# Memory attention of the first layer one step earlier, and two tiles handled by halves

## The chip, the cores and the metric

The kernel runs on one core of a Trainium2 chip. A core has five engines that run side by side and wait for each other by semaphores: TensorE (PE in the profile; its weight loads are listed apart as PEld), VectorE (DVE), ScalarE (ACT), GpSimd (POOL) and SyncE (SP), which here only issues DMAs. TensorE reads its operands from SBUF and writes to PSUM, which has 8 banks of 128 x 512 float32. The metric is the device time of one execution in microseconds, lower is better.

## The reference

Two layers run over a residual stream of 512 tokens with 1024 features. Each layer has a token mixer, a cross-attention of 4 heads into 256 memory tokens beside it, one output projection for both, and a gated MLP with a short causal convolution. Layer 0 mixes by differential attention with 6 heads, layer 1 by gated linear attention. Cut to what the change touches, layer 0:

```python
h = rms_norm(x, attn_norm[i])
proj = h @ w_in_diff[j]                      # q, k, v, mem_q
mix = diff_attention(q, k, v, ...)           # 6 heads, two softmaxes each, o = (p0 - lam * p1) @ v
# memory_cross_attention(mem_q, mem, ...):
kv = rms_norm(mem, mem_norm_g) @ w_kv        # 256 memory tokens -> k, v
q = rms_norm(q, g0) * (64 ** -0.5); k = rms_norm(k, g1)
p = softmax(q @ k.T); cross = p @ v          # 4 heads of 64
x = x + concat([mix, cross]) @ w_out[i]
x = x + conv_ffn(rms_norm(x, ffn_norm[i]), w_up[i], conv_w[i], conv_b[i], w_down[i])
```

All is float32. Large products are made of three passes: each operand is split into a rounded part (hi) and a remainder (lo), and hi·hi, hi·lo and lo·hi are summed in PSUM.

## The kernel before

**Order of the work.** TensorE's instructions run exactly in the order in which the program writes them. The opening (lines 361 to 430) is also in written order on ScalarE, VectorE, GpSimd and SyncE. Everywhere else a planner orders the instructions of the other engines and of the DMA queues by its own estimate of when each becomes ready; an engine then works through its list strictly in that order, so an instruction that waits holds up all behind it.

**The filler.** `Filler` (line 92) holds small units of large projections. `F.fill(us)` takes units off the list for about so many microseconds, so that TensorE has work while a chain of attention runs through the other engines. `F.need(name)` takes units until a mark is reached. A unit of a projection is 6 matmuls (lines 257 to 259) of 512 columns.

**Weights.** SyncE loads weight tiles (line 212), ScalarE casts them to the hi part (line 203), VectorE subtracts for the lo part (line 206). Five such pairs are held at a time, so the cast of a later tile waits for the matmuls that read an earlier one.

**The opening.** The first projection goes by k, an eighth of the 1024 features at a time. For k = 0 one DMA of 128 x 512 float32 on ScalarE's queue (line 374) brings the first weights, VectorE casts them in one instruction (line 401), and x comes and is split in two halves of 256 tokens (lines 376 and 403). For k = 0 the 12 matmuls, four token blocks by three passes, go by pass: hi·hi of all four blocks first (lines 427 to 430).

**Layer 0's attention.** `diff_layer` (line 547) runs 21 steps t (line 689). A step works on one third of a head: steps 0, 3, 6 and so on take query blocks 2 and 0, the next block 1, the next block 3. In a step TensorE does the logits of t (line 615, two banks of the pool "lg"), the products with v of t - 2 (line 653, pool "sm"), a fill, the norms of the next pair of heads when t is 4 or 10 (lines 717 to 719), the turn of t - 1 (transposes, line 172, pool "tp"), pieces of the memory attention, a second fill, and then what the next heads need: `prepare` (line 574) turns queries and keys of a head in steps 5, 6, 11 and 12, `finish` (line 666) turns the output of a head. Each of the pools "lg", "sm", "tp" and "mm" has two banks.

After the logits VectorE adds the bias and finds the maximum (line 620; the bias tile bt comes by DMA, line 606), ScalarE takes the exponential (line 623), VectorE combines the two softmaxes (lines 628 to 631), and after the turn ScalarE copies the transposes out of PSUM (line 641).

**Memory attention.** `MemAttn` (line 483) has four query blocks. `logits(b)` writes two lg banks (line 506); VectorE finds the maxima (line 509), ScalarE the exponentials (line 513), VectorE the quotient (lines 515 and 517). `turn(u)` transposes half a block into a tp bank, copied out by VectorE or ScalarE in turn (line 526). `values(pair)` multiplies with v (line 540, an sm bank) and splits the result (lines 240 and 241). The constant M0 = 7 (line 688) places them: with m = t - M0, logits at m = 0 to 3, turns at m = 1 to 4, two in each, and values at m = 3 and 5. The memory keys are turned once by `keys0` (line 469), at the end of step 6 (line 735), through an lg bank, and copied out by ScalarE (line 475). Step 10 also makes the operands of the second layer's memory projection (lines 700 to 702, splits by lines 240 and 241).

**The end.** The last product of layer 1's MLP is made in tiles of 128 features by 512 tokens. VectorE adds each to the residual (line 995) and SyncE issues the DMA to the output (line 1093).

Of the kernel before, what the change touches and what calls it, by code (L numbers as in the profile page):

```python
# [131 lines left out]
def trunk(ctx, tc, head_d, x_t, mem_t, wpack, cols_a_d, cols_d, conv_d, gate_d, rel_bias, diff_lambda, consts, onehot, out):  # L132
# [12 lines left out]
    def bank(tag):  # L145
        return ps.tile([128, 512], F32, name=f"ps_{tag}", tag=tag)
# [12 lines left out]
    def blk(b, w=128):  # L159
        return slice(w * b, w * b + w)  # L160
# [200 lines left out]
    with tc.tile_pool(name="ini", bufs=1) as ip, tc.manual_schedule(engines={E.Activation, E.DVE, E.Pool, E.SP}):  # L361
        idle = ip.tile([128, 512], F32, name="idle")
        rb = ip.tile([32, 6], F32, name="rb")
        oh = ip.tile([32, 640], F32, name="oh")
        bs = xtile()[:6], xtile()[:6, :128]
        lv = xtile()[:, :256]
        G.memset(idle, 0.0)
        p = bank("tp")
        for n in (512, 320):
            mm(p[:, :n], idle[:, 0:128], idle[:, :n], start=True, stop=True)  # L370


        raws = [ip.tile([128, WTILE], F32, name=f"raw{i}") for i in range(4)]
        A.dma_start(raws[0][:, blk(0, S)], wpack[0, :, blk(0, S)])
        head = ip.tile([128, 32 + S], F32, name="head")
        for c in (slice(0, 32 + S // 2), slice(32 + S // 2, 32 + S)):
            load(head[:, c], head_d[:, c])
        xT[0] = head[:, 32:]
        for k in range(1, KT):
            xT[k] = xtile()  # L380
            load(xT[k], x_t[k])
            load(raws[k // 2][:, blk(k % 2, S)], wpack[k // 2, :, blk(k % 2, S)])
        load(cols_a, cols_a_d)
        at[0] = 4
        load(C[:, 640:768], consts[:, 640:768])
        load(rb, rel_bias)
        load(oh, onehot)
        second = [load_raw(raw_tile(), WTILE) for _ in range(3)]
        load(cols, cols_d)
        load(lv, diff_lambda[0].rearrange("a b -> (a b)").partition_broadcast(128))  # L390
        parts, acc, split_w = [], [None], [None]
        made.append(parts)

        def operands(k):
            if k % 2 == 0:
                split_w[0] = [wp.tile([128, WTILE], F32R, name=n, tag=n, bufs=WB) for n in ("whi", "wlo")]
            c = blk(k % 2, S)
            hi, lo = split_w[0]
            xh[k], xl[k] = split_tiles()
            if k == 0:  # L400
                V.tensor_copy(hi[:, c], raws[0][:, c])
                V.tensor_sub(lo[:, c], raws[0][:, c], hi[:, c].bitcast(F32))
                for t in (blk(0, S // 2), blk(1, S // 2)):
                    split(xh[0][:, t], xl[0][:, t], xT[0][:, t], col(0, head))
            else:
                split(xh[k], xl[k], xT[k], col(k, head))
                split_weights(c, raws[k // 2], hi, lo)
            parts.append((hi[:, c], lo[:, c]))
            squares(xT[k], acc)

        operands(0)
        for k in range(KT):
            if k + 1 < KT:
                operands(k + 1)
            if k == 0:
                second.append(load_raw(raws[0], WTILE))
            if k == 4:
                bias_rows(rb, oh, bs)
            if k == KT - 2:
                make_piece(second, lambda: token_rsqrt("lg", acc[0], NB, r_x[:, 0]))  # L420
                weights(("qk", 0))
                small_vectors()
                for c in range(2):
                    load(bias_d[:, 512 * c:min(512 * c + 512, 640)], bs[c])
            hi, lo = parts[k]
            terms = (xh[k], hi), (xh[k], lo), (xl[k], hi)
            todo = [(b, i) for b in range(NB) for i in range(3)]
            for b, i in sorted(todo, key=lambda bi: bi[1]) if k == 0 else todo:
                xp, w = terms[i]
                mm(first[b], xp[:, blk(b)], w, start=k == 0 and i == 0, stop=k == KT - 1 and i == 2)  # L430

    load(C[:, 0:640], consts[:, 0:640])
    for i in range(4):
# [16 lines left out]
    def mem_kv(l):  # L450
        hs, ls = [None] * KT, [None] * KT
        km = [None]

        def operands():
            if l == 0:
                mem_squares()
            km[0] = xtile().rearrange("p (b n) -> p b n", b=2)
            for k in range(KT):
                if k % 2 == 0:
                    mh, ml = split_tiles()  # L460
                c = blk(k % 2, 256)
                hs[k], ls[k] = mh[:, c], ml[:, c]
                split(hs[k], ls[k], memT[k // 2][:, c], c_mem(l, k))

        def ev(b, p):
            A.activation(km[0][:, b], p[:, :256], AF.Copy, scale=r_mem[:, b:b + 1])
            A.activation(vm[l][:, b], p[:, 256:], AF.Copy, scale=r_mem[:, b:b + 1])

        def keys():
            F.need(f"kv{l}")  # L470
            p = bank("lg")
            for hp in range(2):
                for b in range(2):
                    transpose(p[:, 256 * hp + 128 * b:256 * hp + 128 * b + 128], km[0][:, b, blk(hp)])
            A.activation(kmT[l].rearrange("p a b -> p (a b)"), p, AF.Copy, scale=c_mk(l))
        gemm(hs, ls, 2, ("kv", l), 512, ev,
             (lambda: token_rsqrt("lg", mem_acc[0], 2, r_mem)) if l == 0 else None)
        F.add(0.0, lambda: group_norm(None, km[0], 2, 4, 64))
        F.mark(f"kv{l}")
        return operands, keys  # L480


# [64 lines left out]
    def diff_layer(pool, mix, acc):  # L547
# [137 lines left out]
        F.fill(1.2)  # L685
        prepare(1)
        ma = MemAttn(pool, 0, qm, mix, False)
        M0 = 7
        for t in range(21):
            if t == 0:  # L690
                project_qk(1)
                ops0, keys0 = mem_kv(0)
                gemm(xh, xl, NB, ("v", 1), 512, lambda b, p: A.activation(
                    v12[:, b], p, AF.Copy, scale=r[:, b:b + 1]))
                F.mark("v1")
                project_qk(2)
            if t == 2:
                ops0()
                ma.norm()
            if t == 10:  # L700
                ops1, keys1 = mem_kv(1)
                ops1()
            if t == 16:
                keys1()
            if t == 12:
                load_x(x_t)
                out_proj(0, mix, 0, None)
            if t == 18:
                rest = out_proj(0, mix, 1, acc, 5)
            f = FILL[bisect(STEPS, t)]  # L710
            m = t - M0
            if t < 18:
                logits(t)
            if 0 <= t - 2 < 18:
                values(t - 2)
            F.fill(f)
            if t in (4, 10):
                norms((t + 2) // 6, 0)
                norms((t + 2) // 6, 1)
            if 0 <= t - 1 < 18:  # L720
                turn(t - 1)
            if 1 <= m < 5:
                ma.turn(2 * m - 2)
            if m in (3, 5):
                ma.values(m // 2 - 1)
            if 0 <= m < 4:
                ma.logits(m)
            if t == 20:
                F.flush()
            F.fill(f)  # L730
            if 1 <= m < 5:
                ma.turn(2 * m - 1)
            if t == 3:
                ma.queries()
            if t == 6:
                keys0()
            if t in (5, 6, 11, 12):
                prepare(2 * ((t + 1) // 6) + (t + 1) % 6)
            if t % 3 == 2 and t >= 5:
                finish(t // 3 - 1)  # L740
# [253 lines left out]
    def update(n, p, gain, acc):  # L994
        V.tensor_add(xT[n], xT[n], p)
        if gain is None:
            return
        xh[n], xl[n] = split_tiles()
        split(xh[n], xl[n], xT[n], gain(n))
        squares(xT[n], acc)  # L1000
# [27 lines left out]
    def ffn(pool, l, acc):  # L1028
# [31 lines left out]
        for half, nq in enumerate(HALVES):  # L1060
# [22 lines left out]
            for c in range(4):  # L1083
                pn = bank("lg"), bank("tp")
                parts = weights(("dn", l, base, c))
                for n in range(2):
                    product(pn[n], parts, n, mids)
                for n in range(2):
                    update(2 * c + n, pn[n], (lambda k: c_attn(1, k)) if last and l == 0 else None, acc2)
                    if last and l == 0:  # L1090
                        nc.sync.dma_start(xres[2 * c + n], xT[2 * c + n])
                    if last and l == 1:
                        nc.sync.dma_start(out[2 * c + n], xT[2 * c + n])
# [91 lines left out]
```

## Time and profile before

| | |
|---|---|
| median of 3 runs | 1187.88 us (1187.5 to 1188.62) |
| profiled execution | 1186.74 us |
| its span, first to last instruction | 1185.0 us |
| TensorE busy | 1171.4 us (99%), 5656 matmuls |
| VectorE busy | 756.9 us (64%) |
| ScalarE busy | 546.2 us (46%) |
| DMA | 117.81 MB, mean 99 GB/s |
| mean granted TensorE clock | 0.998 |

How to read the rows: L615 is line 615 of the kernel. A row of the order of time gives start, duration, engine, line, operation, output<-inputs, shapes and the number of instructions merged; in brackets, for how long the engine stood idle before and who ended that. A row of the waits reads "engine, its line <- engine and line waited for: us in total, times, longest". A row of the stretches gives the stretch, its length, then busy time (and instructions) of PE, PEld, DVE, ACT and POOL, the granted clock as a share of full speed, the DMA share and GB/s. A row of DMA issues ends with the size and the median us from issue to landing. Durations of neighbouring matmuls overlap, since they are pipelined.

### The profile page before, as it was taken

How to read it: one execution, taken by the hardware profiler on the slowest of the kernel's cores; microseconds unless marked ns; L12 is line 12 of the kernel's file. 1: busy time of each engine (PE TensorE's matmuls, PEld its weight loads, DVE VectorE, ACT ScalarE, POOL GpSimd, SP SyncE). 2: the span in 40 equal slices, each digit the busy share in tenths (PEclk: the TensorE clock that was granted, in tenths of full speed). 3: DMA queues.
4: the chain of work that ended last, by engine and by line, in shares of the span. 5: the costliest groups of instructions: out<-in, count | busy, mean ns of one | idle time of the engine just before them, and what ended most of it. 6: DMA issues, size and time to landing. Idle time of an engine off the chain costs nothing.

```text
span 1185.0 us, 14743 instructions
## 1 busy us (share of the span) xinstructions
PE 1171.4 (99%) x5656; PEld 966.8 (82%) x5656; DVE 756.9 (64%) x1250; ACT 546.2 (46%) x952; POOL 4.5 (0%) x25
## 2 busy tenths in 40 slices
PE   9999989999999999999999999999999999999998
PEld 7888867888888888888888788988888888888887
DVE  7566686687767435767557746768777643476741
ACT  6676676564434223444437535436443422343420
POOL 0000000000000000000000000000000000000000
PEclk9999999999999999999999999999999999999999
DMA  8432214142322332322341221333233233242231
GB/s 294 126 93 89 80 41 138 49 139 72 124 89 89 107 107 80 116 71 90 119 152 68 72 71 59 110 99 125 72 111 102 76 120 107 71 125 72 89 116 44
DMA packets 39268, 117.81 MB, mean 99 GB/s; under 512 B 4671, under 2 KB 6520, under 8 KB 39198
## 3 DMA queue, kind: packets, MB, share of 16 engines
q1 hardware_dynamic: 39054, 116.62, 30.9%
q8 instruction: 44, 0.72, 0.3%
q10 hardware_dynamic: 144, 0.26, 0.1%
q14 instruction: 26, 0.21, 0.1%
HBM read 112.65 MB, written 4.21 MB: 99 GB/s over the span
## 4 chain that ended last, share of the span: by engine, by line
PE 93%; DVE 3%; ACT 2%; issue 1%; DMA 0%; ACTq 0%; DVEq 0%
PE ps_mm L275 9%; PE ps_mm L276 9%; PE ps_mm L274 9%; PE ps_sm L275 7%; PE ps_sm L274 7%; PE ps_sm L276 7%; PE ps_mm L257 5%; PE ps_mm L259 5%; PE ps_mm L258 5%; PE ps_tp L275 3%; PE ps_tp L274 3%; PE ps_tp L276 3%; PE ps_lg L275 3%; PE ps_lg L276 3%; PE ps_lg L274 3%; PE ps_tp L172 2%
## 5 line engine op out<-in xcount | busy, mean ns | idle before, releaser
L203 ACT CAST whi<-raw 128x1024 fp32r<-128x1024 f32 (+4 forms) x212 | 208.4, 985 | 261.1 <-PE ps_tp L275 131.2
L206 DVE TENSOR_TENSOR wlo<-raw,whi 128x1024 fp32r<-128x1024 f32 (+4 forms) x212 | 241.1, 1140 | 107.5 <-ACT whi L203 106.4
L274 PE MATMUL ps_mm<-xsh,whi 128*128 128x512 f32 x438 | 173.0, 395 | 0.0
L275 PE MATMUL ps_mm<-xsl,whi 128*128 128x512 f32 x438 | 170.6, 390 | 0.2 <-DVE xsl L241 0.2
L276 PE MATMUL ps_mm<-xsh,wlo 128*128 128x512 f32 x438 | 170.7, 390 | 0.0
L274 PE MATMUL ps_sm<-xsh,whi 128*128 128x512 f32 x378 | 147.1, 389 | 0.0
L276 PE MATMUL ps_sm<-xsh,wlo 128*128 128x512 f32 x378 | 147.1, 389 | 0.0
L275 PE MATMUL ps_sm<-xsl,whi 128*128 128x512 f32 x378 | 147.1, 389 | 0.0
L257 PE MATMUL ps_mm<-whi,xsh 128*128 128x512 f32 (+2 forms) x352 | 136.2, 387 | 0.1
L259 PE MATMUL ps_mm<-whi,xsl 128*128 128x512 f32 (+2 forms) x352 | 131.0, 372 | 0.4 <-DVE xsl L241 0.4
L258 PE MATMUL ps_mm<-wlo,xsh 128*128 128x512 f32 (+2 forms) x352 | 130.6, 371 | 0.0
L1045 ACT ACTIVATE cvo<-u,cv 128x512 f32<-128x512 f32 x88 | 71.4, 813 | 121.4 <-DVE u L1043 121.4
L275 PEld LDWEIGHTS ps_mm<-xsl,whi 128*128 128x128 f32 x438 | 82.3, 188 | 17.6 <-DVE xsl L241 0.6
L274 PEld LDWEIGHTS ps_mm<-xsh,whi 128*128 128x128 f32 x438 | 82.3, 188 | 17.4 <-issue 0.5
L276 PEld LDWEIGHTS ps_mm<-xsh,wlo 128*128 128x128 f32 x438 | 82.2, 188 | 17.1
L1046 DVE SCALAR_TENSOR_TENSOR cvo<-u,cv,cvo 128x512 f32<-128x512 f32 x88 | 65.8, 749 | 38.7 <-ACT cvo L1045 38.7
L274 PEld LDWEIGHTS ps_sm<-xsh,whi 128*128 128x128 f32 x378 | 71.0, 188 | 14.8
L275 PEld LDWEIGHTS ps_sm<-xsl,whi 128*128 128x128 f32 x378 | 71.0, 188 | 14.7
L276 PEld LDWEIGHTS ps_sm<-xsh,wlo 128*128 128x128 f32 x378 | 70.9, 188 | 14.7
L257 PEld LDWEIGHTS ps_mm<-whi,xsh 128*128 128x128 f32 x352 | 66.4, 189 | 13.6 <-issue 3.0
L259 PEld LDWEIGHTS ps_mm<-whi,xsl 128*128 128x128 f32 x352 | 66.1, 188 | 12.5 <-DVE xsl L241 0.6
L258 PEld LDWEIGHTS ps_mm<-wlo,xsh 128*128 128x128 f32 x352 | 66.4, 189 | 10.0
(271 smaller groups left out, 1746.4 us busy)
## 6 DMA issues: line engine op xcount, KB each, us to landing
raw<-in_wpack_dram SPq DMA_DIRECT2D x178, 512.0 KB, 3.5
xt<-in_x_t_dram SPq DMA_DIRECT2D x15, 256.0 KB, 6.0
raw<-in_wpack_dram SPq DMA_DIRECT2D x15, 256.0 KB, 3.9
raw<-in_wpack_dram SPq DMA_DIRECT2D x8, 384.0 KB, 3.2
xres<-xt SPq DMA_DIRECT2D x8, 256.0 KB, 2.0
xt<-xres SPq DMA_DIRECT2D x8, 256.0 KB, 3.7
out_dram<-xt SPq DMA_DIRECT2D x8, 256.0 KB, 2.0
bt<-bias_d SPq DMA_DIRECT2D x6, 256.0 KB, 4.4
```

The source lines that it names most:

```text
L172: nc.tensor.transpose(dst, src, ident[:n, :n])
L203: ins = A.copy(hi[:, c], raw[:, c])
L206: V.tensor_sub(lo[:, c], raw[:, c], hi[:, c].bitcast(F32))
L257: mm(p, sh[k][:, blk(b)], hi, start=k == 0, stop=False)
L258: mm(p, sh[k][:, blk(b)], lo, start=False, stop=False)
L259: mm(p, sl[k][:, blk(b)], hi, start=False, stop=k == KT - 1)
L274: mm(p, hi[:, blk(n)], bh, start=i == first, stop=False)
L275: mm(p, hi[:, blk(n)], bl, start=False, stop=False)
L276: mm(p, lo[:, blk(n)], bh, start=False, stop=i == last)
L1045: A.activation(c, u[:, 2:], AF.Identity, scale=cv[l][:, 2, j:j + 1], bias=cv[l][:, 3, j:j + 1])
L1046: V.scalar_tensor_tensor(c, u[:, 1:S + 1], cv[l][:, 1, j:j + 1], c, op0=ALU.mult, op1=ALU.add)
```

## The change

There are four edits. M0 becomes 6, so that each part of the first layer's memory attention stands one step earlier. The keys are turned in the middle of step 6, behind the logits and products of that step and ahead of its first fill, into a bank of the pool "tp" instead of "lg". The first weight tile is loaded by two DMAs of half the columns, both on ScalarE's queue, and cast by two instructions; the first hi·hi passes over token blocks 0 and 1 are made as four matmuls of 256 columns, left halves first (the right halves don't reset the bank). The last output tile is added by two instructions of half the tokens, each followed by its own DMA, the first on SyncE's queue, the second on ScalarE's.

```diff
-        A.dma_start(raws[0][:, blk(0, S)], wpack[0, :, blk(0, S)])
+        for t in (blk(0, S // 2), blk(1, S // 2)):
+            A.dma_start(raws[0][:, t], wpack[0, :, t])
...
             if k == 0:
-                V.tensor_copy(hi[:, c], raws[0][:, c])
+                for t in (blk(0, S // 2), blk(1, S // 2)):
+                    V.tensor_copy(hi[:, t], raws[0][:, t])
...
-            todo = [(b, i) for b in range(NB) for i in range(3)]
-            for b, i in sorted(todo, key=lambda bi: bi[1]) if k == 0 else todo:
+            full, left, right = slice(0, S), blk(0, S // 2), blk(1, S // 2)
+            todo = [(b, i, full) for b in range(NB) for i in range(3)]
+            if k == 0:
+                todo = [(0, 0, left), (1, 0, left), (0, 0, right), (1, 0, right)] + sorted(
+                    [u for u in todo if u[:2] not in ((0, 0), (1, 0))], key=lambda u: u[1])
+            for b, i, t in todo:
                 xp, w = terms[i]
-                mm(first[b], xp[:, blk(b)], w, start=k == 0 and i == 0, stop=k == KT - 1 and i == 2)
+                mm(first[b][:, t], xp[:, blk(b)], w[:, t], start=k == 0 and i == 0 and t is not right,
+                   stop=k == KT - 1 and i == 2)
...
-        def keys():
+        def keys(tag="lg"):
             F.need(f"kv{l}")
-            p = bank("lg")
+            p = bank(tag)
...
-        M0 = 7
+        M0 = 6
...
                 values(t - 2)
+            if t == 6:
+                keys0("tp")
             F.fill(f)
...
-            if t == 6:
-                keys0()
...
                 for n in range(2):
+                    if last and l == 1 and c == 3 and n == 1:
+                        for t, queue in ((blk(0, S // 2), nc.sync), (blk(1, S // 2), nc.scalar)):
+                            V.tensor_add(xT[7][:, t], xT[7][:, t], pn[n][:, t])
+                            queue.dma_start(out[7, :, t], xT[7][:, t])
+                        continue
                     update(2 * c + n, pn[n], (lambda k: c_attn(1, k)) if last and l == 0 else None, acc2)
```

## The prediction

> **What bounds the kernel now.** I read the page first, then TensorE's waits, then busy time by stretch, then the order of time around the longest wait.
>
> ```profile
> span 1185.0 us, 14743 instructions
> PE 1171.4 (99%) x5656; PEld 966.8 (82%) x5656; DVE 756.9 (64%) x1250; ACT 546.2 (46%) x952; POOL 4.5 (0%) x25
> ...
> PE ps_lg L615 <- ACT xt L513: 4.1, 2, 2.9
> ...
> PE ps_lg L615 <- ACT kmT L475: 0.4, 1, 0.4
> ...
> 171.60:180.00 8.40, 4.32 (x18) 3.10 (x17) 7.57 (x18) 4.17 (x14) 0.00 (x0) 0.80 0.15 47
> 178.00:179.00 1.00, 1.00 (x5) 0.84 (x5) 0.87 (x4) 0.79 (x2) 0.00 (x0) 0.50 0.68 249
> ```
>
> TensorE is busy in 1171.4 of 1185.0 us, so only its idle time can be won, 13.6 us at most, and stretches where its clock was low. The one large wait is L615, the token attention's logits, on L513, the memory attention's exponentials: 4.1 us in two pieces. The stretch rows show it around 171.6 to 180.0 (TensorE busy 4.32 of 8.40 us) and the clock granted at 0.50 afterwards. The order of time in that place, TensorE alone:
>
> ```profile
> 128.70 1.13 PE L615 MATMUL ps_lg<-kT,qT 64*128 64x256 f32 x8
> 131.26 1.05 PE L653 MATMUL ps_sm<-v,xt 128*128 128x128 f32 x8
> ...
> 148.59 1.13 PE L506 MATMUL ps_lg<-kmT,xt 64*128 64x256 f32 x8
> ...
> 154.41 0.72 PE L615 MATMUL ps_lg<-kT,qT 64*128 64x128 f32 x8
> ...
> 165.75 1.14 PE L506 MATMUL ps_lg<-kmT,xt 64*128 64x256 f32 x8
> ...
> 171.03 0.60 PE L172 MATMUL ps_tp<-C,xt 128*128 128x128 f32 x4
> 174.57 0.70 PE L615 MATMUL ps_lg<-kT,qT 64*128 64x256 f32 x2 [2.94 <-ACT xt L513]
> 176.41 1.83 PE L615 MATMUL ps_lg<-kT,qT 64*128 64x256 f32 x6 [1.14 <-ACT xt L513]
> 178.16 2.07 PE L653 MATMUL ps_sm<-v,xt 128*128 128x128 f32 x8
> 179.89 0.57 PE L257 MATMUL ps_mm<-whi,xsh 128*128 128x512 f32 x1
> ```
>
> The shapes tell the steps: 128.70 is step 8, 154.41 step 10, 174.57 step 11. L506 at 165.75 is the last memory logits, in step 10; the logits of step 11 need its two lg banks. Why those come free so late:
>
> ```profile
> 151.90 0.48 ACT L513 ACTIVATE xt<-ps_lg,nmm 128x256 f32<-128x256 f32 x1
> ...
> 175.80 0.47 ACT L513 ACTIVATE xt<-ps_lg,nmm 128x256 f32<-128x256 f32 x1
> ...
> 172.78 0.68 DVE L509 TENSOR_REDUCE nmm<-ps_lg 128x2 f32<-128x512 f32 x1
> 173.38 1.21 DVE L314 TENSOR_TENSOR ks<-ks,rs_y 128x1024 f32<-128x1024 f32 x1
> 174.63 0.67 DVE L509 TENSOR_REDUCE nmm<-ps_lg 128x2 f32<-128x512 f32 x1
> ```
>
> In step 10 the maximum L509 starts 7.0 us after L506 (165.75 to 172.78), its second half behind L314 of the norms of pair 2, and the last exponential ends at 176.27: 10.5 us after L506. The same chain one step earlier took 3.8 us (148.59 to 152.38), and step 10's logits came at 154.41, 2.0 us after it. So step 10, with norms and the splits of the second memory projection, is where VectorE has no room.
>
> **The change, part by part.** M0 from 7 to 6 moves every memory logits, turn and product one step up. Their instructions stay as many: on TensorE L506, L172 and L540, on VectorE L509, L515, L517, half the copies L526 and the second halves of the splits L241, on ScalarE L513, the other copies and L240. They issue no DMA and nothing on POOL; SP's queue keeps its order of weight and bias loads unless the planner shifts it. On a busy TensorE a moved matmul costs nothing by itself; what counts is waits.
>
> *Step 11's wait.* The last memory logits now stand in step 9, in the place of the row at 148.59, with the second fill and a turn before step 10's logits; chain 3.8 us, cover 5.8 us. The stall: the turn ends at 171.63 (171.03+0.60), the next projection matmul starts at 179.89, 8.26 us, for work that took 1.13+1.05 = 2.18 us in step 8. Lost: 6.1 us, of which 4.08 idle and 2.0 low clock. I take -6.1. What is late next: the fourth head's turned queries, which wait for L314 (ended 174.59; its keys were turned at 185.07, and will be some 6 us sooner). That leaves about 5 us, enough even if the projection that feeds the norms, pushed behind the moved products and logits (1.97 and 1.14, rows of their kind below and above), ends 3 us later.
>
> *The keys.* In step 6 they were turned at the step's end into an lg bank:
>
> ```profile
> 115.64 0.60 PE L172 MATMUL ps_lg<-C,xt 128*128 128x128 f32 x4
> ...
> 117.78 0.42 DVE L620 CUSTOM_DVE_ANT_0 xt<-ps_lg,bt 128x256 f32<-128x256 f32 x1 [6.93 <-PE ps_lg L615]
> ```
>
> Step 7's logits waited 0.4 us for that bank. Now the keys take a tp bank ahead of the fill; the memory projection that they read was done in the step before, a whole fill lies between their eviction and the first memory logits, and the turn of the step takes the other tp bank. -0.4 us; should the keys' eviction queue behind the step's exponentials, the same fill covers it. The new first memory logits find VectorE idle for 6.93 us in this step: 0.
>
> *Steps 11 and 12 without their cover.* The products L540 of the second half leave step 12 for step 11, and two turns leave step 11.
>
> ```profile
> 104.73 0.66 PE L172 MATMUL ps_tp<-C,o 128*128 128x128 f32 x4 [0.34 <-ACT qT L582]
> ...
> 185.07 0.66 PE L172 MATMUL ps_tp<-C,ks 128*128 128x128 f32 x4 [0.53 <-ACT xt L526]
> ...
> 190.88 0.60 PE L172 MATMUL ps_tp<-C,xt 128*128 128x128 f32 x4
> 191.41 1.97 PE L540 MATMUL ps_sm<-xt,vm 128*64 128x128 f32 x32
> ...
> 196.02 0.66 PE L172 MATMUL ps_tp<-C,ks 128*128 128x128 f32 x4 [0.62 <-ACT xt L641]
> ...
> 191.08 0.83 ACT L203 CAST whi<-raw 128x768 fp32r<-128x768 f32 x1 [0.52 <-PE ps_mm L259]
> ...
> 195.40 0.56 ACT L641 COPY xt<-ps_tp 128x512 f32<-128x512 f32 x1
> ...
> 191.95 0.96 DVE L206 TENSOR_TENSOR wlo<-raw,whi 128x768 fp32r<-128x768 f32 x1 [0.40 <-ACT whi L203]
> 192.82 0.55 DVE L620 CUSTOM_DVE_ANT_0 xt<-ps_lg,bt 128x384 f32<-128x384 f32 x1
> ```
>
> In step 11 the 0.53 us behind the copy L526 goes, and as in step 5 the turn of o then waits 0.34 for L582: -0.2. In step 12 the turn at 190.88 is copied out only at 195.40, since ScalarE first casts a weight tile that waits for the fill's matmuls, VectorE subtracts it (L206), and only then takes L620; the keys at 196.02 stand 5.14 us behind the turn. The products filled 1.9 of that (1.97 by their row, less what overlaps). Without them the same chain leaves 0.62+1.9 = 2.5 us idle: +1.9. If the planner lets L620 go ahead, the 0.62 goes too: -0.6. The cast and L206 wait for TensorE's own fill, which moves with everything, so I take the order as it stands: +1.9.
>
> *First weights and last output.*
>
> ```profile
> 4.07 0.51 ACT L240 ACTIVATE xsh<-head 128x256 fp32r<-128x256 f32 x1 [2.06 <-DMA head<-in_head_dram]
> 4.33 0.43 DVE L401 CAST whi<-raw 128x512 fp32r<-128x512 f32 x1 [3.47 <-DMA raw<-in_wpack_dram]
> 4.91 1.19 PE L430 MATMUL ps_mm<-whi,xsh 128*128 128x512 f32 x2 [0.46 <-DVE whi L401]
> ...
> 2.32 0.34 PEld L370 LDWEIGHTS ps_tp<-idle 128*128 128x128 f32 x1 [0.52 <-issue]
> ...
> 1181.28 0.69 DVE L995 TENSOR_TENSOR xt<-xt,ps_tp 128x512 f32<-128x512 f32 x1 [6.11 <-PE ps_tp L276]
> 1181.99 0.33 SPq L1093 DMA_DIRECT2D out_dram<-xt  x1
> out_dram<-xt SPq DMA_DIRECT2D x4, 256.0 KB, 2.0
> ```
>
> A half tile is cast in about half of 0.43 us, but the first matmul also needs the split of x, done at 4.58; it was 4.91, so at most -0.33. Against it, four half matmuls with four weight loads (0.34 us each while slow, 1.36 together) replace two that took 1.19: +0.2. I take -0.1; the extra load is issued by ScalarE, which has nothing to compute before 4.07. At the end the first half goes out while VectorE adds the second, which still ends near 1181.97; what is saved is half of the last tile's movement. Of 2.0 us to landing that is between 0 and 1.0, and ScalarE's queue, which has carried nothing since the start, could cost as much as its issue, 0.33. I take -0.3.
>
> Sum: -6.1-0.4-0.2+1.9-0.1-0.3 = -5.2 us. The profiled execution took 1186.74 (span 1185.0 and 1.74 around it), which gives 1181.5; the median of the runs shown is 1.14 higher, 1187.88, and gives **1182.7 us**, the forecast. Its own range is 1181.0 to 1184.0, a tail or start term off and one us either way in step 12.
>
> **The rivals.** *L620 goes ahead in step 12* (needs the bias tile and its place in VectorE's order before the two L206). For it: everything L620 needs is there at 192; against: the planner put it behind. -5.2-2.5 = -7.7: 1180.2 us.
>
> *The 2.5 us gap lowers the clock.* In step 11 2.94 and 1.14 us idle, with 0.70 of work between, were followed by 0.50 granted, 2.0 us lost. If 2.5 us suffices, +2.0: 1184.7 us. The Trainium skill, TensorE: Matmul & The Clock Gate, section Why this matters for your kernels, says to avoid idle gaps of more than about 3 us; by that rule a gap of 2.5 us would leave the clock alone. The trace can't settle it: its one low stretch stands behind 2.94 and 1.14 us together.
>
> *VectorE stays the bound.* It was busy 7.57 of the 8.40 us around the stall. If its backlog, not the lg banks, sets when pair 2's norms end, the turn of the fourth head's queries waits instead. It decides from norms 5 us later than now, and 9 us later would eat 4.0 of the gain: 1186.7 us, no difference. Against it: the reductions, quotients and copies of the last memory logits leave just this stretch.
>
> ```profile
> 143.00:154.00 11.00, 11.00 (x67) 8.83 (x66) 7.00 (x20) 6.42 (x21) 0.00 (x0) 1.00 0.00 0
> ```
>
> *Slower: step 9 becomes the new step 10.* The second projection's splits, made at the head of step 10, slip ahead of the memory logits' reductions. From a chain of 5.8 us on step 10's logits wait. With 10.5 us, as now, the loss is 4.7 idle and 2.0 clock, which with the rest gives 1189.4; slower by 0.2% from about 11.4 us. Against it: VectorE and ScalarE, 7.00 and 6.42 of 11.00 us busy around step 9, are far from full there.
>
> *It doesn't do what it says:* step 9 has the same wait by other means; then only start, keys and end remain, -0.8, and step 12's +1.9: 1189.0.
>
> **How the numbers follow.** Chances: forecast 0.46, L620 ahead 0.20, clock 0.12, VectorE bound 0.10, slower 0.08, no effect 0.04. A difference of 0.2%, 2.4 us, is about what can be told from none. Forecast, L620 and clock are faster; VectorE's bound is within 0.2%; the last two straddle +2.4. Faster 0.78, same 0.14, slower 0.08. The range reaches from 1179.2 (L620 ahead, the end worth 1.0 more) to 1186.7; above it lie the last two, 0.12.
>
> **What would show it.** Right: no L513 wait above 1 us on L615; no granted clock below 1.00 between 165 and 180; the kmT row gone; L540 twice before step 12; a wait of L172 on L641 near 2.5 us in step 12; last output in two issues. Wrong: a wait of L172 on L314 or L582 in step 11, L615 on L513 in step 10, or 0.50 granted after step 12's gap.

## The result, and the profile after

The changed kernel takes 1183.15 us (median of 6 executions, 1182.12 to 1185.46) against 1187.95 us for the kernel before on the same chip (6 executions, 1186.88 to 1188.7). The ratio is 0.9964, with a 95% interval from 0.9951 to 0.9976: faster by about 0.36%. The forecast was 1182.7 us. The profiled execution took 1182.33 us, 4.41 less than that of before.

The new edits push most line numbers down. What was L615 (logits of the token attention) is L622, L620 is L627 (bias and maximum), L623 is L630 (exponentials), L641 is L648 (copy of the turned weights), L653 is L660 (products with v), L582 is L589 (eviction of turned queries and keys), L506 is L513 (memory logits), L513 is L520 (their exponentials), L540 is L547 (their products), L475 is L482 (copy of the turned memory keys), L466 and L467 are L473 and L474 (evictions of the memory projection), L430 is L436 (matmuls of the opening). L172, L203, L206 and L314 keep theirs.

The head of the page of the changed kernel:

```profile
span 1180.5 us, 14752 instructions
```

TensorE's waits (total, times, longest), and under them busy time by stretch:

```profile
PE ps_tp L172 <- ACT xt L648: 2.9, 1, 2.9
...
PE ps_lg L622 <- ACT kmT L482: 0.4, 1, 0.4
```

```profile
165.00:180.00 15.00, 15.00 (x105) 12.23 (x104) 14.34 (x37) 11.92 (x34) 0.15 (x1) 1.00 0.39 124
171.60:180.00 8.40, 8.40 (x72) 6.68 (x71) 8.37 (x24) 5.32 (x15) 0.15 (x1) 1.00 0.25 81
```

The wait of 4.1 us on the memory attention's exponentials is gone from the list. In the stretch from 171.6 to 180.0, where TensorE was busy for 4.32 of 8.40 us, it is now busy throughout and at full clock. VectorE is busy for 8.37 of the same 8.40 us, and TensorE does not wait for it. In place of the old wait a wait of 2.9 us on the copy L648 leads. TensorE's order of time around it, and what ScalarE did meanwhile:

```profile
171.97 0.63 PE L172 MATMUL ps_tp<-C,xt 128*128 128x128 f32 x4
172.53 1.13 PE L622 MATMUL ps_lg<-kT,qT 64*128 64x256 f32 x8
...
174.51 0.48 PE L257 MATMUL ps_mm<-whi,xsh 128*128 128x512 f32 x1
...
176.28 1.97 PE L547 MATMUL ps_sm<-xt,vm 128*64 128x128 f32 x32
...
179.68 0.60 PE L172 MATMUL ps_tp<-C,qs 128*128 128x128 f32 x4
...
181.87 0.66 PE L172 MATMUL ps_tp<-C,o 128*128 128x128 f32 x4 [1.16 <-ACT qT L589]
182.46 1.14 PE L622 MATMUL ps_lg<-kT,qT 64*128 64x192 f32 x12
...
186.85 0.60 PE L172 MATMUL ps_tp<-C,xt 128*128 128x128 f32 x4
...
188.67 0.60 PE L172 MATMUL ps_tp<-C,qs 128*128 128x128 f32 x4
192.19 0.66 PE L172 MATMUL ps_tp<-C,ks 128*128 128x128 f32 x4 [2.92 <-ACT xt L648]
```

```profile
180.41 0.82 ACT L203 CAST whi<-raw 128x768 fp32r<-128x768 f32 x1
181.13 0.69 ACT L589 ACTIVATE qT<-ps_tp,cols 128x512 f32<-128x512 f32 x1
...
187.05 0.84 ACT L203 CAST whi<-raw 128x768 fp32r<-128x768 f32 x1 [0.55 <-PE ps_mm L259]
188.87 0.47 ACT L473 ACTIVATE xt<-ps_mm,r_mem 128x256 f32<-128x256 f32 x1 [0.98 <-PE ps_mm L259]
...
189.60 0.61 ACT L630 ACTIVATE xt<-xt,nmd 128x384 f32<-128x384 f32 x1
...
191.56 0.57 ACT L648 COPY xt<-ps_tp 128x512 f32<-128x512 f32 x1
```

Step 11's logits (172.53) and products follow the turn (171.97) with no wait, the fill starts at 174.51, and the memory products L547 come in step 11 (176.28). In step 12 the turn of the weights (186.85) and that of the new queries (188.67) fill both tp banks, so the turn of the new keys waits until L648 has emptied one. Ahead of L648, ScalarE's list has the cast L203, the eviction L473 and step 12's exponentials L630, and the first two wait for TensorE's own fill (L259).

The start, and the end:

```profile
4.33 1.47 PE L436 MATMUL ps_mm<-whi,xsh 128*128 128x256 f32 x4
...
8.24 0.39 PE L436 MATMUL ps_mm<-whi,xsh 128*128 128x512 f32 x1
...
1177.18 0.75 DVE L1098 TENSOR_TENSOR xt<-xt,ps_tp 128x256 f32<-128x256 f32 x2 [6.11 <-PE ps_tp L276]
1177.63 0.33 SPq L1099 DMA_DIRECT2D out_dram<-xt  x1
1177.96 0.35 ACTq L1099 DMA_DIRECT2D out_dram<-xt  x1
```

The first matmul is 0.58 us earlier (4.33 against 4.91), the second feature block 0.03 us (8.24 against 8.27). The last add starts 3.32 us before the end of the span; before it was 3.72 us.

### The profile page after: what moved, and what is told of

Its sections match the earlier page's. It is cut to its first block, busy times and chain, and to the rows that moved or that the text cites. A ratio compares the mean times of both kernels' runs of the same rounds, so it can differ in the third digit from the quotient of the medians.

```text
span 1180.5 us, 14752 instructions
## 1 busy us (share of the span) xinstructions
PE 1169.2 (99%) x5658; PEld 965.8 (82%) x5658; DVE 757.1 (64%) x1252; ACT 546.2 (46%) x952; POOL 4.6 (0%) x25
## 4 chain that ended last, share of the span: by engine, by line
PE 93%; DVE 3%; ACT 2%; issue 1%; POOL 0%; DVEq 0%; ACTq 0%; POOLq 0%
PE ps_mm L275 9%; PE ps_mm L276 9%; PE ps_mm L274 9%; PE ps_sm L274 7%; PE ps_sm L275 7%; PE ps_sm L276 7%; PE ps_mm L257 5%; PE ps_mm L259 5%; PE ps_mm L258 5%; PE ps_tp L275 3%; PE ps_tp L274 3%; PE ps_tp L276 3%; PE ps_lg L275 3%; PE ps_lg L276 3%; PE ps_lg L274 3%; PE ps_tp L172 2%
## 5 line engine op out<-in xcount | busy, mean ns | idle before, releaser
L203 ACT CAST whi<-raw 128x1024 fp32r<-128x1024 f32 (+4 forms) x212 | 208.5, 986 | 258.8 <-PE ps_tp L275 130.7
L206 DVE TENSOR_TENSOR wlo<-raw,whi 128x1024 fp32r<-128x1024 f32 (+4 forms) x212 | 241.2, 1140 | 107.0 <-ACT whi L203 106.0
L259 PE MATMUL ps_mm<-whi,xsl 128*128 128x512 f32 (+2 forms) x352 | 131.1, 372 | 0.4 <-DVE xsl L241 0.4
L259 PEld LDWEIGHTS ps_mm<-whi,xsl 128*128 128x128 f32 x352 | 66.1, 188 | 12.5 <-DVE xsl L241 0.6
```

Of the source, the lines that this page charges most:

```text
L203: ins = A.copy(hi[:, c], raw[:, c])
L206: V.tensor_sub(lo[:, c], raw[:, c], hi[:, c].bitcast(F32))
L259: mm(p, sl[k][:, blk(b)], hi, start=False, stop=k == KT - 1)
```

## The experiments

What was to be settled: which of the four edits carries the gain; what holds the copy L648 in step 12; what the gap there costs; and why the six executions spread over 3.3 us. Medians are of all executions of a kernel; ratios are to the kernel before on the same chip.

**The attention edits alone, the ends alone, the keys alone.** The first kernel is the one before with these edits:

```diff
-        def keys():
+        def keys(tag="lg"):
...
-            p = bank("lg")
+            p = bank(tag)
...
-        M0 = 7
+        M0 = 6
...
+            if t == 6:
+                keys0("tp")
             F.fill(f)
...
-            if t == 6:
-                keys0()
```

> The attention edits alone (M0 = 6, keys turned early through a tp bank), start and end as before. If steps 11 and 12 carry the change: no wait of the logits on L513, a wait of 2.5 to 3.0 us of the turned keys on the copy of the turn in step 12, a span of about 1180.9 us (the change's 1180.5 and the 0.4 us of its end given back), and about 4 us less than before. If instead the halved start or end had set the gain, a span within 1 us of 1185.

It took 1184.41 us (1183.06 to 1185.34), ratio 0.9969, 0.9957 to 0.9982. Its waits are those of the changed kernel, 2.92 us in step 12 among them. The profiled execution spans 1183.5 us and not 1180.9: the clock fell behind that wait (rows below), and already in step 5 it was 1.2 us later than before (the queries' turn at 104.53 against 103.35), which comes from the opening, left as it was. The second has the other edits of the change only:

```diff
-        A.dma_start(raws[0][:, blk(0, S)], wpack[0, :, blk(0, S)])
+        for t in (blk(0, S // 2), blk(1, S // 2)):
+            A.dma_start(raws[0][:, t], wpack[0, :, t])
...
+                    if last and l == 1 and c == 3 and n == 1:
+                        for t, queue in ((blk(0, S // 2), nc.sync), (blk(1, S // 2), nc.scalar)):
...
```

> The halved first weights and the halved last output alone, M0 = 7 and the keys as before. Expected: the 4.1 us wait of the logits on L513 is there as before, the second feature block's matmuls start within 0.1 us of 8.27 us although the first matmul starts near 4.3 instead of 4.91, and from the last addition's start to the end it takes 3.3 instead of 3.7 us: span about 1184.6. The rival, in which starting 0.6 us earlier is kept to the end, gives 1184.0.

It took 1187.29 us (1186.6 to 1187.83, 10 executions), ratio 0.9993, 0.9984 to 1.0002, which is 0.8 us and no difference that this measurement can tell. Two expectations failed: the second block starts at 8.57 us, later than before and not within 0.1 of 8.27 (more on this in the last section), and the profiled span is 1185.5 us, not 1184.6. The third is the first without the change of M0:

> Only the keys' turn moved ahead of step 6's first fill and into a tp bank, M0 = 7. The prediction took 0.4 us for it; then the 0.4 us wait of the logits on the keys' eviction would be gone. The rival, from the trace of the change, is that this wait belongs to the second layer's keys, which still go through lg near 215 us: then it stays, and the span is within 0.2 us of before but for the noise of a run.

It took 1188.02 us in its one execution, too few to tell a difference of 0.4 us, but its waits settle it. With M0 at 7 the 4.1 us on L513 are still there, and so is the keys' row:

```profile
PE ps_lg L615 <- ACT kmT L475: 0.4, 1, 0.4
```

So M0 carries nearly all of the gain. The keys bring nothing, and the reason is that the prediction read this row as step 7's. The wait lies some 100 us later: the token attention's logits of step 16 wait for a bank through which the second layer's memory keys, left as they were, have just been turned. First the kernel before, then the changed one, TensorE's order of time:

```profile
215.71 0.71 PE L615 MATMUL ps_lg<-kT,qT 64*128 64x128 f32 x6 [0.36 <-ACT kmT L475]
```

```profile
211.60 0.71 PE L622 MATMUL ps_lg<-kT,qT 64*128 64x128 f32 x6 [0.36 <-ACT kmT L482]
```

**The products back in step 12.** The changed kernel with its second half of the memory products L547 one step later, where they were before:

```diff
-            if m in (3, 5):
-                ma.values(m // 2 - 1)
+            if m in (3, 6):
+                ma.values(m // 3 - 1)
```

> The change, with the second products of the memory attention put back from step 11 to step 12, between the turn and the second fill. If the lost cover makes the 2.92 us wait in step 12, it falls by 1.9 to about 1.0 us, the span is near 1178.6, and no execution shows a clock below 1.000, so that the median comes to about 1180.4 with all runs within 1 us. If the wait is set by something that moves along with TensorE, it stays near 2.9 us and the time with it.

1180.39 us (1179.73 to 1181.19), ratio 0.9936, 0.9924 to 0.9949; below the changed kernel by 2.8 us in the medians, and by 1.9 us where its executions at full clock are taken (1182.33). TensorE's turns of keys in steps 11 and 12:

```profile
178.40 0.63 PE L172 MATMUL ps_tp<-C,ks 128*128 128x128 f32 x4 [0.78 <-DVE rcd L636]
...
189.60 0.65 PE L172 MATMUL ps_tp<-C,ks 128*128 128x128 f32 x4 [0.89 <-ACT xt L648]
```

The wait of step 12 falls from 2.92 to 0.89 us, 2.0 us for a row of 1.97 us. It confirms that the products were cover there, at the price that the prediction gave. In step 11, with the products gone, the wait of 1.16 us on L589 goes, and one of 0.78 us on VectorE appears: the new keys wait for their norm L314, which ends at 178.26 (the row names the short L636 right behind it). That is a small form of the rival in which VectorE stays the bound. Not as expected, two of the five executions have a mean clock of 0.999, and they spread over 1.5 us.

**A gap filled with idle work.** The changed kernel with ten extra matmuls between step 12's turned queries and its keys. They go into a free mm bank and their result is used by nothing.

```diff
-                A.activation(dst, p, AF.Copy, scale=g)
-                t2.append(dst)
+                A.activation(dst, p, AF.Copy, scale=g); spare = bank("mm") if h == 5 and nm == "qT" else None
+                t2.append(dst); [mm(spare, mix[0][0][:, 0:128], mix[0][0], start=True, stop=True) for _ in range(10 if spare is not None else 0)]
```

> The change, with ten matmuls of 512 columns that compute nothing of use put between the turned queries and the turned keys of step 12, into a spare mm bank: about 2.3 us of the 2.92 us gap is filled with idle work, and no useful instruction moves. If the gap's own length is all it costs, the time and its spread stay as they are (three executions near 1182.3, two near 1185.4 in six). If a gap of 2.92 us brings the clock down in some executions only, the fast level stays near 1182.3, the executions near 1185.4 and the clocks of 0.997 are gone, and the median falls to about 1182.3.

1182.55 us (1181.98 to 1183.19), ratio 0.9951, 0.9939 to 0.9964. The keys now wait for 0.63 us instead of 2.92:

```profile
192.45 0.66 PE L172 MATMUL ps_tp<-C,ks 128*128 128x128 f32 x4 [0.63 <-ACT xt L648]
```

Useless work cannot bring the keys forward (192.45 against 192.19), and it does not. But all five executions have a mean granted clock of 1.000, where the changed kernel has 0.997 in two of six (1185.41 and 1185.46 us) and 1.000 in the three lowest. The other kernels with such a gap in step 12 (2.92 or 3.14 us) agree with the changed one: below 1.000 are four of five executions with the attention edits alone, three of five with the casts held back and eight of nine with the evictions moved (both below). So the gap costs its length always, and in many executions low clock behind it.

A clock row of the changed kernel in such an execution isn't there, since its profiled one was at full clock. The profiled executions of two of the others show what follows the gap. Busy time and, after POOL, the granted clock, first of the attention edits alone (gap until 193.35), then of the kernel with the casts held back (gap until 192.44):

```profile
193.40:196.70 3.30, 3.30 (x17) 2.74 (x18) 1.85 (x7) 2.59 (x6) 0.00 (x0) 0.50 0.10 41
```

```profile
191.50:198.30 6.80, 5.86 (x25) 4.92 (x26) 2.92 (x12) 4.80 (x19) 0.00 (x0) 0.50 0.00 0
```

The clock is halved for 3.4 us in the one and for 6.8 us in the other, and 1.00 ahead of it and behind. If TensorE does half the work at half the clock, an estimate of the loss is 1.7 or 3.4 us. That is near the steps between the changed kernel's levels of 1182.3, 1183.8 and 1185.4 us.

**More fill in step 12.** 2.6 us more of the output projection ahead of the turn:

```diff
-            F.fill(f)
+            F.fill(f + 2.6 if t == 12 else f)
```

> The change, with 2.6 us more of the output projection taken into step 12's second fill, ahead of the turned queries. If cover is what step 12 lacks, the wait of 2.92 us falls to 0 to 0.6 us, the span to about 1178 and the median to about 1180 with no clock below 1.000. If those units are missed later, in steps 17 to 20, a wait of the same size shows up there and the time stays.

1182.6 us (1180.95 to 1183.64), ratio 0.995, 0.9938 to 0.9963. The wait moves instead of going, as the second case of the expectation has it. TensorE's order of time, and a stretch behind it:

```profile
191.49 0.66 PE L172 MATMUL ps_tp<-C,ks 128*128 128x128 f32 x4 [0.18 <-ACT xt L648]
...
221.30 0.71 PE L660 MATMUL ps_sm<-v,xt 128*128 128x128 f32 x4 [1.89 <-ACT xt L648]
```

```profile
222.70:226.00 3.30, 3.30 (x12) 2.61 (x11) 0.20 (x1) 0.00 (x0) 0.00 (x0) 0.50 0.02 5
```

The keys wait 0.18 us, but some 30 us later, near the end of the attention, products wait 1.89 us for the copy of a later turn, and the clock is halved for 3.4 us soon after; in the changed kernel TensorE is busy throughout from 220 to 225 us, at full clock. The filler's work is finite: what is taken in step 12 is missing where a later chain needs it.

**What makes the copy late.** The prediction named the cast L203, the subtraction L206 behind it and L627 behind that. The first kernel takes just these away: the casts of the third and fourth weight tile of the output projection are held back.

```diff
-            split_weights(slice(0, n * w), raw, hi, lo, len(made) == 2)
+            split_weights(slice(0, n * w), raw, hi, lo, len(made) in (2, 9, 10))
```

> The change, with the casts of the third and fourth weight tiles of the first output projection held back to their place in the program, so that VectorE's bias and maximum of step 12's logits no longer stand behind two subtractions that wait for TensorE's fill. TensorE's order is untouched. If that place in VectorE's and ScalarE's lists makes the wait of 2.92 us in step 12, it falls below 0.6 us and the span to about 1178. If the copy of the turn is late for another reason, the wait stays above 2 us. If the weights then come late, L274 waits for them in steps 15 to 18.

1184.06 us (1182.31 to 1185.57), ratio 0.9958, 0.9945 to 0.9972: no gain over the changed kernel. L627 went ahead as meant, and yet the keys waited just as long. The order of time of this kernel, VectorE, ScalarE and TensorE:

```profile
184.21 0.55 DVE L627 CUSTOM_DVE_ANT_0 xt<-ps_lg,bt 128x384 f32<-128x384 f32 x1
...
189.12 0.47 ACT L473 ACTIVATE xt<-ps_mm,r_mem 128x256 f32<-128x256 f32 x1 [5.61 <-PE ps_mm L259]
...
189.85 0.61 ACT L630 ACTIVATE xt<-xt,nmd 128x384 f32<-128x384 f32 x1
...
192.44 1.11 PE L172 MATMUL ps_tp<-C,ks 128*128 128x128 f32 x4 [2.92 <-ACT xt L648]
```

ScalarE stood idle for 5.61 us before L473, the eviction of the second layer's memory projection, which waits for the second fill's last matmul. The exponentials behind it had their input 5 us before they began (the first of the four L627 ended at 184.76, L630 began at 189.85). The second kernel therefore puts those evictions behind the copy and leaves the casts where they were:

```diff
-            A.activation(km[0][:, b], p[:, :256], AF.Copy, scale=r_mem[:, b:b + 1])
-            A.activation(vm[l][:, b], p[:, 256:], AF.Copy, scale=r_mem[:, b:b + 1])
+            with tc.issue_after(made_by[11].ins) if l and b else ExitStack():
+                A.activation(km[0][:, b], p[:, :256], AF.Copy, scale=r_mem[:, b:b + 1]), A.activation(vm[l][:, b], p[:, 256:], AF.Copy, scale=r_mem[:, b:b + 1])
...
-            A.copy(wT[:, :n], pt[:, :n])
+            made_by[t] = A.copy(wT[:, :n], pt[:, :n])
```

> The change, with only the last two evictions of the second layer's memory projection put behind the copy of step 11's turn in ScalarE's list; the weight casts stay ahead of step 12's exponentials. Holding the casts back alone left the wait at 2.92 us, with the exponentials then behind these evictions. If two things stand in front of the exponentials, each of which waits for TensorE's fills of this step, opening one alone changes nothing: a wait of 2.5 to 3 us stays. If the evictions alone were the cause, the wait falls to 0.6 us or less.

1184.86 us (1182.43 to 1185.74, 9 executions), ratio 0.9972, 0.9963 to 0.9982: no gain either. Now casts alone stand before the exponentials, and the wait is 3.14 us:

```profile
189.67 1.04 ACT L203 CAST whi<-raw 128x1024 fp32r<-128x1024 f32 x1 [0.99 <-PE ps_mm L259]
190.62 0.61 ACT L630 ACTIVATE xt<-xt,nmd 128x384 f32<-128x384 f32 x1
```

A cast that in the changed kernel stands behind the exponentials (192.61 there) has taken the place of the evictions. It is not what holds them: the first L627, behind the two earlier casts and their L206, ended only at 190.14. Without it the exponentials could have begun 0.5 us sooner, by estimate, and most of the wait would remain.

The third does both, and puts step 12's evictions of turned queries and keys behind the copy too:

```diff
-            split_weights(slice(0, n * w), raw, hi, lo, len(made) == 2)
+            split_weights(slice(0, n * w), raw, hi, lo, len(made) in (2, 9, 10))
...
+            with tc.issue_after(made_by[11].ins) if l and b else ExitStack():
...
-                A.activation(dst, p, AF.Copy, scale=g)
-                t2.append(dst)
+                with tc.issue_after(made_by[11].ins) if h == 5 else ExitStack():
+                    A.activation(dst, p, AF.Copy, scale=g), t2.append(dst)
```

> The change, with everything that waits for step 12's fills put behind the exponentials and the copy of the turn: the casts of two weight tiles held back, and the evictions of the memory projection and of the new queries and keys put behind the copy. No matmul moves. If these places in the lists of ScalarE and VectorE are the whole cause, the wait of 2.92 us goes, to below 0.6 us, the span comes to about 1177.8, the median to about 1179.7 and no execution shows a clock below 0.999. If the lost cover were needed whatever the order, a wait above 1.5 us stays.

1179.47 us (1179.22 to 1181.02), ratio 0.9934, 0.9921 to 0.9946: 3.7 us below the changed kernel in the medians, and 0.66% below the one before. Where only executions at full clock are taken, three of each, it is 1179.37 against 1182.33: 3.0 us, the length of the gap. ScalarE, then TensorE:

```profile
184.33 0.62 ACT L630 ACTIVATE xt<-xt,nmd 128x384 f32<-128x384 f32 x1 [1.29 <-DVE nmd L627]
...
187.26 0.59 ACT L648 COPY xt<-ps_tp 128x512 f32<-128x512 f32 x1 [0.85 <-PE ps_tp L172]
```

```profile
188.46 0.60 PE L172 MATMUL ps_tp<-C,qs 128*128 128x128 f32 x4
188.89 0.60 PE L172 MATMUL ps_tp<-C,ks 128*128 128x128 f32 x4
```

The exponentials begin 5.3 us sooner, the copy is done before the turns that need its bank, and the keys follow the queries without a wait. No matmul was moved. Two things stood in front of the exponentials, each enough to hold them, so that taking away one brought nothing. Whether the evictions of queries and keys had to go behind the copy as well was not tried by itself.

**Both remedies together.** The last kernel has these holds and the products back in step 12:

> Both remedies: the order on ScalarE as in the experiment with everything put behind the copy, and the second products back in step 12. Each alone is expected to bring 2 to 3 us; together they can only take what is left, at most the 0.89 us that the products left in step 12, since step 11's 0.78 us behind the norms stays: a span of 1177.0 to 1178.0 and a median near 1179.5.

1181.24 us (1180.16 to 1181.99), ratio 0.9944, 0.9931 to 0.9958: less gain than from the holds alone, and not the 1179.5 us expected. The intervals of the two ratios overlap; the order of time shows where the difference lies. ScalarE:

```profile
187.82 0.38 ACT L240 ACTIVATE mxh<-ps_sm 128x256 fp32r<-128x256 f32 x1 [6.38 <-PE ps_sm L547]
188.10 0.61 ACT L630 ACTIVATE xt<-xt,nmd 128x384 f32<-128x384 f32 x1
```

The split L240 of the late products now stands before the exponentials, and ScalarE idles for 6.38 us until TensorE has made them. It is the same fault with a third instruction: the new keys again wait, for 0.89 us, and in step 11 for 0.78 us on VectorE. With the chain in time, the cover is no longer wanted.

## Why the prediction was right, and where it was not

*Step 11's wait, -6.1: right, measured -6.4.* No wait on L520 is left and the clock stays at 1.00 from 165 to 180. The cause was the right one as well: in step 9 the chain from the last memory logits (L513 at 152.68) to the end of the last exponential (157.05) took 4.4 us, against 3.8 forecast and 10.5 before in step 10, and step 10's logits came at 158.50. And VectorE is fuller there than before (8.37 of 8.40 us) and TensorE doesn't mind, so the two lg banks set the wait, not VectorE's backlog.

*The keys, -0.4: wrong, 0.* The step that failed is "Step 7's logits waited 0.4 us for that bank": the row of the waits names no time, and it was placed in step 7 for its name alone. The same row stands unchanged in the kernel with the keys alone and in the changed one, and stands at step 16's logits, behind the second layer's keys.

*Step 11's turn of o, -0.2: wrong, +0.2.* The 0.53 went, but the new wait is 1.16, not 0.34. The 0.34 was step 5's, where nothing stood before the eviction L582. Here ScalarE casts a weight tile first (L203 at 180.41, 0.82 us) and evicts at 181.13. What the prediction listed as a sign against it, a wait on L582 in step 11, is there in this small form. The prediction also overlooked that step 12's logits had waited behind these turns, and no longer do. In the kernel before:

```profile
183.94 0.60 PE L172 MATMUL ps_tp<-C,qs 128*128 128x128 f32 x4
...
186.51 1.14 PE L615 MATMUL ps_lg<-kT,qT 64*128 64x192 f32 x12 [0.19 <-ACT kT L582]
```

*Step 12, +1.9: near in size, incomplete in cause.* The gap is 2.92 us against 2.5 forecast; by starts the step loses 2.1. The prediction said "the same chain leaves 0.62+1.9 = 2.5 us idle", and putting the products back took 2.0 off. But the chain it named, cast, L206, L620, is one of two: with L627 early the evictions L473 held the exponentials just as long. The rival "L620 goes ahead" would, for that reason, not have brought its 2.5 us even if it had happened; that rival's condition was too weak.

*First weights, -0.1: not told, and last output, -0.3: right.* The second feature block starts at 8.24, before at 8.27, but that is one execution of each. In the nine kernels here with the halved opening, one profiled execution each, it starts between 7.46 and 8.57, so the opening changes by more from one execution to the next than the term is worth. The last output measured -0.40. The kernel with these two edits alone gives 0.8 us, within what can't be told from none.

*The sum.* The terms can be read from start to start in the two profiled executions, since durations of neighbouring matmuls overlap. From the turn at the end of step 10 to the fill behind step 11's products, 8.86 us (171.03 to 179.89) became 2.54 (171.97 to 174.51). That is -6.3, and another -0.1 lies in the fill behind, which began at low clock. From step 11's turn of queries to step 12's logits, 2.57 us (183.94 to 186.51) became 2.78 (179.68 to 182.46): +0.2. From step 12's turn of weights to its keys, 5.14 us became 5.34 (186.85 to 192.19), although 1.9 of products had left: +2.1. Together this is -4.1, and step 16's logits do begin 4.11 us sooner (211.60 against 215.71). With -0.40 at the end that makes the 4.5 us by which the span shrank. Against the forecast of -5.2, the keys and the turn of o were too favourable by 0.4 each, step 12 by 0.2 and the first weights by 0.1, while step 11's wait was worth 0.3 more and the last output 0.1 more.

For the profiled execution the sum gave 1181.5 us, and it took 1182.33. The median came closer to its forecast, 1183.15 against 1182.7, and that is luck. The prediction carried over the 1.14 us by which the median of before lies above the profiled execution. Behind step 11's stall the profiled execution of before had 3.4 us at half clock; the profiled one of the kernel with the keys alone, which has the same stall, had 6.8. Of the 39 executions of before measured with the experiments, 33 have a mean clock of 0.997, the profiled one 0.998. So most probably the 1.14 us is longer low clock behind a stall that the change removed. The changed kernel's median lies 0.82 us above its profiled execution for another reason, low clock in some of its executions.

*The clock rival, 1184.7: right in some executions.* The prediction treated it as one way or the other for the kernel. It is decided anew in each execution: 1182.1 to 1182.5 us at 1.000, 1183.8 at 0.999, 1185.4 and 1185.5 at 0.997. The median lies between these. The Trainium skill, TensorE: Matmul & The Clock Gate, section Why this matters for your kernels, warns of gaps of more than about 3 us; by the rows above, 2.92 us is enough in some executions, and the last section has shorter ones. The same page, Part 1: The HAM clock gate, says that the gate watches a window of about 3.4 us that runs freely and doesn't start with the kernel. The traces agree: the low stretches last 3.4 or 6.8 us, and the same gap costs clock in some executions only.

*The slower rival and the one without effect: not seen.* Neither a wait of step 10's logits on L520 nor one in step 11 is in the trace. VectorE as the bound came only in the two kernels with the products back in step 12, at 0.78 us.

## What to carry to other kernels

A wait that a profile names ends with one instruction, but the list of the engine that issues it may hold several instructions that each wait for the same late event: read everything that stands between the input's arrival and the late instruction, and remove all of it in one kernel; here each trial alone showed nothing. Where an engine with an ordered list is the late one, moving its early-placed, late-ready instructions behind the chain (-3.7 us here in the medians, with no matmul moved) brought more than extra fill for TensorE (-0.6), which is finite and brings the late copy no nearer. Putting the late products back as cover brought about as much (-2.8; the intervals overlap), but the two together brought less than the order alone. Before a small wait is put down to a step, find its time; a name that fits is not a place.

## What the runs showed of the hardware that was not expected

A gap of 2.92 us on TensorE lowered the granted clock in some executions of the same kernel and not in others; with the gap filled to 0.63 us, in none of five. Shorter idle time can do it as well. In the kernel with more fill a gap of 1.89 us ended at 221.30, and from 222.6 to 226.0 the clock was at 0.50. In the profiled execution of the kernel with all holds (mean clock 0.999, 1180.49 us) step 12 has no gap, and the clock was halved far from it, at the start of the second layer. TensorE's order of time ahead of it, and the stretch:

```profile
613.19 0.39 PE L259 MATMUL ps_mm<-whi,xsl 128*128 128x272 f32 x1 [0.37 <-DVE xsl L241]
613.79 1.05 PE L348 MATMUL ps_sm<-C,xt 128*128 128x1 f32 x8 [0.21 <-DVE xt L342]
```

```profile
616.10:619.40 3.30, 3.30 (x16) 3.30 (x16) 1.18 (x8) 0.64 (x2) 0.00 (x0) 0.50 0.05 16
```

Only 0.37 and 0.21 us of idle time and eight matmuls of one column stand there. So an execution at 0.999 doesn't prove that step 12's gap was the place, and no run here shows how much idle time is safe.

In all eight profiled executions whose clock fell, it was at 0.50 for 3.4 us (five of them) or 6.8 us (three).

At the start, the first matmuls run at about half speed for a time that differs between executions of the same opening. First the kernel with the ends alone, then the one with the products back in step 12:

```profile
6.32 1.02 PE L436 MATMUL ps_mm<-wlo,xsh 128*128 128x512 f32 x2
7.18 0.63 PE L436 MATMUL ps_sm<-wlo,xsh 128*128 128x512 f32 x2
...
8.57 0.39 PE L436 MATMUL ps_mm<-whi,xsh 128*128 128x512 f32 x1
```

```profile
5.12 0.63 PE L436 MATMUL ps_sm<-whi,xsh 128*128 128x512 f32 x2
...
7.46 0.39 PE L436 MATMUL ps_mm<-whi,xsh 128*128 128x512 f32 x1
```

Their first matmuls begin together (4.17 and 4.19), but two matmuls of 512 columns still take 1.02 us at 6.32 in the one, and 0.63 us from 5.12 on in the other. In the changed kernel the first matmul began 0.58 us sooner than before, and both kernels ran at the faster pace from 6.4 us on. A sooner start is worth something only where the slow time happens to end early. The stretch row shows a granted clock of 1.00 for this time, so it doesn't show the slow pace. The kernel with the ends alone:

```profile
4.00:8.00 4.00, 4.00 (x13) 3.11 (x13) 3.46 (x8) 3.47 (x7) 0.00 (x0) 1.00 1.00 333
```
